# Strided attention: dense weights over four heads, values masked on GpSimd, 2 KiB store runs

## The chip, the cores and the metric

The kernel runs on one core of one Trainium2 chip. The metric is device time in microseconds of the whole program, median over its executions. The profile lists the instructions of TensorE (PE, 880 matmuls in the kernel before, with its 880 weight loads as PEld), VectorE (DVE, 144), ScalarE (ACT, 103), GpSimd (POOL, 23) and SyncE (SP) apart, and the packets of 16 DMA engines, which in the kernel before read 25.95 MB from HBM and wrote 25.17 MB to it. "Span" is the time from the first to the last instruction of the profiled execution; it is about 1.8 us shorter than the device time here.

## The reference

Every query attends to 16 fixed key positions, every 64th row of K and V:

```python
batch, heads, seq, dim = (8, 12, 1024, 64)
attend_positions = np.arange(0, seq, stride)            # stride = 64: 16 keys
scores = np.einsum('bhqd,bhkd->bhqk', q, k) * scale     # scale = 1/sqrt(64)
weights = np.exp(scores - np.max(scores, axis=-1, keepdims=True))
weights = weights / (np.sum(weights, axis=-1, keepdims=True) + 1e-10)
result[:, :, i, :] = np.einsum('bhqk,bhkd->bhqd', weights, v)[:, :, 0, :]
```

Q and the result are float32, 25.2 MB each. The arithmetic is small; nearly all traffic is one read of Q and one write of the result.

## The kernel before

The 96 (batch, head) pairs are done in 24 groups of four heads. A group's Q is one DMA of 1 MiB, each partition holding 32 rows (8 KiB); its result is one DMA of 1 MiB. Loads run 11 groups ahead (`QBUFS`), and nine output buffers (`OBUFS`) hold results on their way out. All DMAs are issued by SP, in the order of the code.

```python
def scores(g):                      # [cut: the four score matmuls into sc]
    w = wt[g] = w_bufs[g % 3]       # zeroed once; half of each block stays zero
    for a in range(2):
        wa = w[64 * a : 64 * a + 64]
        nc.scalar.activation(
            out=_ap_with(wa, [wa.ap[0], [P, 8], [1, 2], [2, 32]], extra_offset=64 * a),
            in_=sc[64 * a : 64 * a + 64].rearrange("p (t x q) -> p t x q", t=8, x=2),
            func=AF.Exp, bias=0.0, scale=scale,
        )

def outputs(g, c):                  # four times a group
    ps = psum_o.tile([P, 2, 2, 2 * D], FP32, name="o_ps", tag="o")
    for i in range(2):
        nc.tensor.matmul(ps[:, :, i], lhsT=wt[g][:, 2 * c + i],
                         rhs=v_bd[:, g // 2, g % 2].rearrange("p s d -> p (s d)"), ...)
    nc.vector.tensor_tensor(out=out_sb[g][:, :, 4 * c : 4 * c + 4], in0=ps, ... rec[g] ..., op=ALU.mult)

def store(g):                       # per partition: two runs of 16 rows = 4 KiB, one read of 8 KiB
    o = out_sb[g]
    _copy(nc,
        _ap_with(out, [[16 * D, P], [2 * SD, 2], [1, 16 * D]], g * HG * SD),
        _ap_with(o, [o.ap[0], [1, 1], [1, 32 * D]]))

for g in range(NG):                 # steady loop
    sums(g); outputs(g, 0); outputs(g, 1)
    if g + 1 < NG: scores(g + 1)
    outputs(g, 2)
    if g + 2 < NG: transposes(g + 2, 0)
    outputs(g, 3)
    if g + 2 < NG: transposes(g + 2, 1)
    store(g)
    if g + QBUFS < NG: load(g + QBUFS)
```

The softmax here doesn't subtract the row's maximum and nothing guards it: scores larger than these inputs give would overflow.

Of the kernel before, what the change touches and what calls it, by code (L numbers as in the profile page):

```python
# [11 lines left out]
FP32 = mybir.dt.float32  # L12
BF16 = mybir.dt.bfloat16
I16 = mybir.dt.int16
AF = mybir.ActivationFunctionType
ALU = mybir.AluOpType


def _ap_with(ap: bass.AP, new_ap, extra_offset: int = 0) -> bass.AP:
    return dataclasses.replace(  # L20
        ap, ap=[list(p) for p in new_ap], offset=ap.offset + extra_offset
    )
# [26 lines left out]
def kernel(  # L49
# [8 lines left out]
    nc = tc.nc  # L58

    B, H, S, D = Q.shape  # L60
    NK = S // stride
    scale = 1.0 / math.sqrt(D)

    P = 128
    HG = 4
    NG = B * H // HG
    NC = NG // 2
    SD = S * D
# [4 lines left out]
    const = ctx.enter_context(tc.tile_pool(name="const", bufs=1))  # L73
    qn_pool = ctx.enter_context(tc.tile_pool(name="qn", bufs=QBUFS))
    out_pool = ctx.enter_context(tc.tile_pool(name="outsb", bufs=OBUFS))
    qt_pool = ctx.enter_context(tc.tile_pool(name="qt", bufs=2))
    rec_pool = ctx.enter_context(tc.tile_pool(name="rec", bufs=2))
    psum_qt = ctx.enter_context(tc.tile_pool(name="pqt", bufs=2, space=bass.MemoryType.PSUM))
    psum_sc = ctx.enter_context(tc.tile_pool(name="psc", bufs=2, space=bass.MemoryType.PSUM))
# [23 lines left out]

    identity = const.tile([P, P], BF16, name="identity")
    make_identity(nc, identity)
    id_v = identity.rearrange("p (c b a k) -> p c b a k", c=2, b=2, a=2)

    perm_k = const.tile([P, 2, 2, 2, NK], BF16, name="perm_k")

    perm_v = const.tile([P, 2, 2, 2, 2, NK], BF16, name="perm_v")  # L110
    for c in range(2):
        for a in range(2):
            nc.gpsimd.tensor_copy(out=perm_k[:, c, a], in_=id_v[:, c, :, a])
    k_dup = const.tile([P, NC, 2, D], BF16, name="k_dup")
    for e in range(2):
        nc.gpsimd.tensor_copy(out=k_dup[:, :, e], in_=k_raw)  # L116
    for c in range(2):
        for a in range(2):
            for e in range(2):
                nc.gpsimd.tensor_copy(  # L120
                    out=perm_v[:, c, a, :, e], in_=id_v[:, c, :, a]
                )
    v_bf = const.tile([P, NC, D], BF16, name="v_bf")
    nc.gpsimd.tensor_copy(out=v_bf, in_=v_raw)  # L124

    k_t = const.tile([P, NC, 2, 4, 2, NK], BF16, name="k_t")
    nc.vector.memset(k_t, 0.0)  # L127
    w_bufs = []
    for i in range(3):
        w = const.tile([P, 8, P], BF16, name=f"w{i}")  # L130
        nc.vector.memset(w, 0.0)
        w_bufs.append(w)


    iota_p = const.tile([P, 1], I16, name="iota_p")
    nc.gpsimd.iota(iota_p, pattern=[[0, 1]], base=0, channel_multiplier=1)  # L136
    slot_i = const.tile([P, 1], I16, name="slot_i")
    nc.vector.tensor_scalar(  # L138
        out=slot_i, in0=iota_p, scalar1=4, scalar2=3,
        op0=ALU.logical_shift_right, op1=ALU.bitwise_and,  # L140
    )
    slot_f = const.tile([P, 1], FP32, name="slot_f")
    nc.vector.tensor_copy(out=slot_f, in_=slot_i)
    col4 = const.tile([P, 4], I16, name="col4")
    nc.gpsimd.iota(col4, pattern=[[1, 4]], base=0, channel_multiplier=0)
    s_sel = const.tile([P, 4], BF16, name="s_sel")
    nc.vector.tensor_scalar(
        out=s_sel, in0=col4, scalar1=slot_f, scalar2=None, op0=ALU.is_equal
    )
    mask = const.tile([P, 4], FP32, name="mask")  # L150
    nc.vector.tensor_scalar(
        out=mask, in0=col4, scalar1=slot_f, scalar2=None, op0=ALU.is_equal
    )


    pk = perm_k.rearrange("p c a b k -> p (c a b k)")
    for n in range(NC // 4):
        kp = psum_o.tile([P, 4, 2, 4, NK], FP32, name="kp", tag="o")
        for i in range(4):
            nc.tensor.matmul(  # L160
                kp[:, i], lhsT=k_dup[:, 4 * n + i].rearrange("p e d -> p (e d)"),
                rhs=pk, start=True, stop=True,
            )
        for e in range(2):
            h = slice(64 * e, 64 * e + 64)
            nc.scalar.copy(  # L166
                k_t[h, 4 * n : 4 * n + 4, :, :, e].rearrange("p n c s k -> p (n c s) k"),
                kp[h].rearrange("p n c s k -> p (n c s) k"),
            )

    v_bd = const.tile([P, NC, 2, 4, D], BF16, name="v_bd")
    for n in range(2):
        for c in range(2):
            vp = psum_sc.tile([P, NC // 2, D], FP32, name="vp", tag="sc")
            nc.tensor.matmul(  # L175
                vp, lhsT=perm_v[:, c].rearrange("p a b e k -> p (a b e k)"),
                rhs=v_bf[:, 6 * n : 6 * n + 6], start=True, stop=True,
            )
            for s in range(4):
                nc.vector.tensor_scalar(  # L180
                    out=v_bd[:, 6 * n : 6 * n + 6, c, s], in0=vp,
                    scalar1=mask[:, s : s + 1], scalar2=None, op0=ALU.mult,
                )

    qt, wt, rec, out_sb = {}, {}, {}, {}

    def transposes(g, x):
        if x == 0:
            qt[g] = qt_pool.tile([P, 2, 8, P], BF16, name="qt", tag="qt")
        ps = psum_qt.tile([P, 8, P], BF16, name="qt_ps", tag="qt_ps")  # L190
        qb = qn[g].bitcast(BF16)
        for i in range(8):
            nc.tensor.transpose(  # L193
                ps[:, i],
                _ap_with(qb, [qb.ap[0], [2, P]], extra_offset=(8 * x + i) * 2 * P + 1),
                identity,
            )
        nc.scalar.copy(qt[g][:, x], ps)  # L198

    def scores(g):  # L200
        sc = psum_sc.tile([P, 512], FP32, name="sc", tag="sc")
        q = qt[g]
        kt = k_t[:, g // 2, g % 2].rearrange("p s e k -> p (s e k)")
        for j in range(4):
            a, b = divmod(j, 2)
            nc.tensor.matmul(  # L206
                sc[32 * j : 32 * j + 32],
                lhsT=kt[:, 32 * j : 32 * j + 32],
                rhs=_ap_with(
                    q, [q.ap[0], [P, 8], [8 * P, 2], [1, 32]],  # L210
                    extra_offset=32 * (2 * b + a),
                ),
                start=True, stop=True, tile_position=(0, 32 * j),
            )
        w = wt[g] = w_bufs[g % 3]
        for a in range(2):
            wa = w[64 * a : 64 * a + 64]
            nc.scalar.activation(  # L218
                out=_ap_with(wa, [wa.ap[0], [P, 8], [1, 2], [2, 32]], extra_offset=64 * a),
                in_=sc[64 * a : 64 * a + 64].rearrange("p (t x q) -> p t x q", t=8, x=2),  # L220
                func=AF.Exp, bias=0.0, scale=scale,
            )

    def sums(g):
        sm = psum_s.tile([P, 2, 8, 2], FP32, name="sm", tag="sm")
        for i in range(8):
            nc.tensor.matmul(  # L227
                sm[:, :, i], lhsT=wt[g][:, i], rhs=s_sel, start=True, stop=True
            )
        rec[g] = rec_pool.tile([P, 2, 16], FP32, name="rec", tag="rec")  # L230
        nc.vector.reciprocal(rec[g], sm.rearrange("p b i e -> p b (i e)"))  # L231

    def outputs(g, c):
        if c == 0:
            out_sb[g] = out_pool.tile([P, 2, 16, D], FP32, name="out_sb", tag="out_sb")
        ps = psum_o.tile([P, 2, 2, 2 * D], FP32, name="o_ps", tag="o")
        for i in range(2):
            nc.tensor.matmul(  # L238
                ps[:, :, i], lhsT=wt[g][:, 2 * c + i],
                rhs=v_bd[:, g // 2, g % 2].rearrange("p s d -> p (s d)"),  # L240
                start=True, stop=True,
            )
        nc.vector.tensor_tensor(  # L243
            out=out_sb[g][:, :, 4 * c : 4 * c + 4],
            in0=ps.rearrange("p b i (e d) -> p b (i e) d", e=2),
            in1=rec[g][:, :, 4 * c : 4 * c + 4].unsqueeze(3).to_broadcast([P, 2, 4, D]),
            op=ALU.mult,
        )

    def store(g):  # L250
        o = out_sb[g]
        _copy(
            nc,
            _ap_with(out, [[16 * D, P], [2 * SD, 2], [1, 16 * D]], g * HG * SD),
            _ap_with(o, [o.ap[0], [1, 1], [1, 32 * D]]),
        )

    for g in range(2):
        for x in range(2):
            transposes(g, x)  # L260
    scores(0)
    for g in range(NG):
        sums(g)
        outputs(g, 0)
        outputs(g, 1)
        if g + 1 < NG:
            scores(g + 1)
        outputs(g, 2)
        if g + 2 < NG:
            transposes(g + 2, 0)  # L270
        outputs(g, 3)
        if g + 2 < NG:
            transposes(g + 2, 1)
        store(g)
        if g + QBUFS < NG:
            load(g + QBUFS)
# [35 lines left out]
```

## Time and profile before

| | before |
|---|---|
| device time, median | 130.34 us (130.26 to 130.61, 4 runs) |
| span of the profiled run | 128.5 us |
| bytes moved, mean rate | 51.26 MB, 399 GB/s |
| busy: PE, DVE, ACT, POOL | 54%, 65%, 67%, 4% |
| last compute instruction ends | about 114 us |

First the page of the kernel before: the span in 40 slices. A digit is the busy share of the 16 DMA engines in tenths, and below it is the rate that they reached.

```profile
span 128.5 us, 2215 instructions
...
DMA  2999989999899899999999999999998999999980
GB/s 57 351 398 418 449 367 490 388 423 439 339 421 487 357 441 439 413 434 449 383 467 426 393 459 428 393 469 421 405 469 357 416 434 416 421 428 421 434 337 23
DMA packets 7722, 51.26 MB, mean 399 GB/s; under 512 B 3872, under 2 KB 3872, under 8 KB 3872
```

The engines are 80% busy or more, mostly over 90%, from the second slice to the third from last. The queue part of the same page (packets, megabytes, share of 16 engines' span) has one data queue, and two small ones that carry instructions.

```profile
q1 hardware_dynamic: 7712, 51.12, 96.3%
q8 instruction: 7, 0.11, 0.4%
q14 instruction: 3, 0.02, 0.0%
```

The table of stretches of the same trace: per stretch the busy time of each engine, then PE's granted clock, the DMA share and the rate.

```profile
core 0: us, PE busy (x) PEld busy (x) DVE busy (x) ACT busy (x) POOL busy (x), PEclk, DMA share, GB/s
60.00:70.00 10.00, 6.29 (x85) 4.51 (x82) 7.65 (x13) 8.44 (x10) 0.00 (x0) 1.00 1.04 440
110.00:115.00 5.00, 1.41 (x16) 0.89 (x16) 3.82 (x7) 0.83 (x2) 0.00 (x0) 0.80 1.02 424
115.00:120.00 5.00, 0.00 (x0) 0.00 (x0) 0.00 (x0) 0.00 (x0) 0.00 (x0) 0.50 1.01 423
120.00:125.00 5.00, 0.00 (x0) 0.00 (x0) 0.00 (x0) 0.00 (x0) 0.00 (x0) 0.50 0.92 385
125.00:128.50 3.50, 0.00 (x0) 0.00 (x0) 0.00 (x0) 0.00 (x0) 0.00 (x0) 0.50 0.09 37
```

The DMA share stays at 1.0 when compute has ended (115 to 120 us), at 423 GB/s, against 440 and 424 GB/s in the two stretches above it. The chain of waits tells another story if it is read alone:

```profile
ACT 60%; PE 13%; DVE 5%; DMA 3%; POOL 3%; issue 2%; ACTq 1%; DVEq 0%; POOLq 0%
ACT qt L198 34%; ACT w L218 26%; PE sc L206 8%; DVE v_bd L180 3%; DMA k_raw<-in_K_dram 3%; PE qt_ps L193 2%; PE o_ps L238 2%; DVE out_sb L243 1%; POOL k_dup L116 1%; POOL perm_v L120 1%; PE sm L227 1%; POOL v_bf L124 1%; ACTq L307 1%; DVEq 
```

It follows ACT because it goes from each instruction to what released it, and loads that landed early release nothing (the list of waits has no wait of a compute engine for a load of Q). It does not say that ACT limits the time: on the chain one group follows the other every 3.94 us, while its load and store take the DMA engines about 4.95 us (an estimate: 2.097 MB at 424 GB/s). The groups of instructions behind it (busy time, mean ns, idle time before and its releaser):

```profile
L243 DVE TENSOR_TENSOR out_sb<-o_ps,rec 128x512 f32<-128x512 f32 x96 | 63.3, 688 | 15.3 <-PE o_ps L238 12.9
L198 ACT COPY qt<-qt_ps 128x1024 bf16<-128x1024 bf16 x48 | 46.2, 1015 | 5.2 <-PE qt_ps L193 4.7
L218 ACT ACTIVATE w<-sc 64x512 bf16<-64x512 f32 x48 | 35.4, 737 | 13.2 <-PE sc L206 12.9
```

Last, two lines on SP. Its timeline (start us, us, what) has the first store:

```profile
25.18 0.63 SPq L34 DMA_DIRECT2D out_dram<-out_sb  x1
```

Its list of waits (us in total, times, longest us) has the wait for the last stores, at the end of the program:

```profile
SPq L307 <- DMA out_dram<-out_sb: 12.6, 1, 12.6
```

### The profile page before, as it was taken

The numbers are of one execution on the slowest core, as the hardware profiler recorded it, in microseconds if no ns is written. First come the engines' busy times: TensorE is split into PE (matmuls) and PEld (weight loads), VectorE is DVE, ScalarE is ACT, GpSimd is POOL, SyncE is SP. The second block draws the span as 40 slices with busy tenths as digits, with TensorE's granted clock in tenths as the row PEclk, the third lists the DMA queues.
The fourth block names the chain that finished last, engine by engine and source line by source line (L and its number), as shares of the span: only waits on it lengthen the run. The fifth ranks groups of instructions, "written<-read, shape, count | busy, mean of one in ns | idle before, by whom it ended". The sixth has DMA issues, their size and how long they took to land.

```text
span 128.5 us, 2215 instructions
## 1 busy us (share of the span) xinstructions
PE 69.4 (54%) x880; PEld 51.1 (40%) x880; DVE 83.7 (65%) x144; ACT 86.3 (67%) x103; POOL 5.1 (4%) x23
## 2 busy tenths in 40 slices
PE   0071665975656866558766578665687655510000
PEld 0040542754445654445544456443465444300000
DVE  6229963787677777787777877877877778750000
ACT  2163294988889888898888898888988888400000
POOL 4470000000000000000000000000000000000000
PEclk9999997799999999999999999999999999955555
DMA  2999989999899899999999999999998999999980
GB/s 57 351 398 418 449 367 490 388 423 439 339 421 487 357 441 439 413 434 449 383 467 426 393 459 428 393 469 421 405 469 357 416 434 416 421 428 421 434 337 23
DMA packets 7722, 51.26 MB, mean 399 GB/s; under 512 B 3872, under 2 KB 3872, under 8 KB 3872
## 3 DMA queue, kind: packets, MB, share of 16 engines
q1 hardware_dynamic: 7712, 51.12, 96.3%
q8 instruction: 7, 0.11, 0.4%
q14 instruction: 3, 0.02, 0.0%
HBM read 25.95 MB, written 25.17 MB: 398 GB/s over the span
## 4 chain that ended last, share of the span: by engine, by line
ACT 60%; PE 13%; DVE 5%; DMA 3%; POOL 3%; issue 2%; ACTq 1%; DVEq 0%; POOLq 0%
ACT qt L198 34%; ACT w L218 26%; PE sc L206 8%; DVE v_bd L180 3%; DMA k_raw<-in_K_dram 3%; PE qt_ps L193 2%; PE o_ps L238 2%; DVE out_sb L243 1%; POOL k_dup L116 1%; POOL perm_v L120 1%; PE sm L227 1%; POOL v_bf L124 1%; ACTq L307 1%; DVEq L307 0%; PE vp L175 0%
## 5 line engine op out<-in xcount | busy, mean ns | idle before, releaser
L243 DVE TENSOR_TENSOR out_sb<-o_ps,rec 128x512 f32<-128x512 f32 x96 | 63.3, 688 | 15.3 <-PE o_ps L238 12.9
L198 ACT COPY qt<-qt_ps 128x1024 bf16<-128x1024 bf16 x48 | 46.2, 1015 | 5.2 <-PE qt_ps L193 4.7
L218 ACT ACTIVATE w<-sc 64x512 bf16<-64x512 f32 x48 | 35.4, 737 | 13.2 <-PE sc L206 12.9
L238 PE MATMUL o_ps<-v_bd,w 128*128 128x256 bf16 x192 | 33.4, 278 | 0.6 <-DVE out_sb L243 0.6
L193 PE MATMUL qt_ps<-identity,qn 128*128 128x128 bf16 x384 | 30.7, 227 | 0.2 <-ACT qt L198 0.2
L193 PEld LDWEIGHTS <-qn 128*128 128x128 bf16 x384 | 27.0, 102 | 3.9 <-issue 2.6
L206 PE MATMUL sc<-qt,k_t 128*32 128x512 bf16 x96 | 9.8, 395 | 24.5 <-ACT qt L198 24.5
L238 PEld LDWEIGHTS <-w 128*128 128x128 bf16 x192 | 14.3, 98 | 6.9 <-issue 6.2
L206 PEld LDWEIGHTS <-k_t 128*32 128x32 bf16 x96 | 4.4, 93 | 29.3 <-issue 29.2
L231 DVE RECIPROCAL rec<-sm 128x32 f32<-128x32 f32 x24 | 8.6, 358 | 9.0 <-PE sm L227 9.0
L227 PE MATMUL sm<-s_sel,w 128*128 128x4 bf16 x192 | 8.5, 166 | 6.9 <-ACT w L218 6.9
L227 PEld LDWEIGHTS <-w 128*128 128x128 bf16 x192 | 6.4, 96 | 11.0 <-ACT w L218 11.0
L180 DVE TENSOR_SCALAR v_bd<-vp,mask 128x384 bf16<-128x384 f32 x16 | 8.5, 608 | 0.1
L166 ACT CAST k_t<-kp 64x512 bf16<-64x512 f32 x6 | 3.5, 579 | 3.6 <-PE kp L160 3.5
L160 PE MATMUL kp<-perm_k,k_dup 128*128 128x128 bf16 x12 | 1.5, 312 | 6.7 <-POOL k_dup L116 6.7
L175 PE MATMUL vp<-v_bf,perm_v 128*128 128x384 bf16 x4 | 1.8, 490 | 4.6 <-DVE v_bd L180 4.1
L160 PEld LDWEIGHTS <-k_dup 128*128 128x128 bf16 x12 | 1.2, 145 | 6.7 <-POOL k_dup L116 6.7
L138 DVE TENSOR_SCALAR slot_i<-iota_p 128x1 int16<-128x1 int16 x1 | 0.2, 156 | 4.7 <-POOL iota_p L136 4.7
L166 ACT ACT_TABLE_LOAD x1 | 1.3, 1283 | 2.5 <-DVE k_t L127 2.5
L127 DVE MEMSET k_t<- 128x1536 uint32 x1 | 1.3, 1338 | 1.1 <-PEq L293 1.1
L175 PEld LDWEIGHTS <-perm_v 128*128 128x128 bf16 x4 | 0.5, 127 | 3.7 <-issue 3.7
L116 POOL CAST k_dup<-k_raw 128x768 bf16<-128x768 f32 x2 | 1.6, 827 | 3.0 <-DMA k_raw<-in_K_dram 3.0
(15 smaller groups left out, 6.0 us busy)
## 6 DMA issues: line engine op xcount, KB each, us to landing
qn<-in_Q_dram SPq DMA_DIRECT2D x24, 1024.0 KB, 19.0
out_dram<-out_sb SPq DMA_DIRECT2D x24, 1024.0 KB, 19.5
k_raw<-in_K_dram SPq DMA_DIRECT2D x1, 384.0 KB, 4.3
v_raw<-in_V_dram SPq DMA_DIRECT2D x1, 384.0 KB, 5.4
```

What stands on the lines that cost most here:

```text
L116: nc.gpsimd.tensor_copy(out=k_dup[:, :, e], in_=k_raw)
L160: nc.tensor.matmul(kp[:, i], lhsT=k_dup[:, 4 * n + i].rearrange("p e d -> p (e d)"), rhs=pk, start=True, stop=True,)
L166: nc.scalar.copy(k_t[h, 4 * n : 4 * n + 4, :, :, e].rearrange("p n c s k -> p (n c s) k"), kp[h].rearrange("p n c s k -> p (n c s) k"),)
L180: nc.vector.tensor_scalar(out=v_bd[:, 6 * n : 6 * n + 6, c, s], in0=vp, scalar1=mask[:, s : s + 1], scalar2=None, op0=ALU.mult,)
L193: nc.tensor.transpose(ps[:, i], _ap_with(qb, [qb.ap[0], [2, P]], extra_offset=(8 * x + i) * 2 * P + 1), identity,)
L198: nc.scalar.copy(qt[g][:, x], ps)
L206: nc.tensor.matmul(sc[32 * j : 32 * j + 32], lhsT=kt[:, 32 * j : 32 * j + 32], rhs=_ap_with(q, [q.ap[0], [P, 8], [8 * P, 2], [1, 32]], ext ...
L218: nc.scalar.activation(out=_ap_with(wa, [wa.ap[0], [P, 8], [1, 2], [2, 32]], extra_offset=64 * a), in_=sc[64 * a : 64 * a + 64].rearrange( ...
L227: nc.tensor.matmul(sm[:, :, i], lhsT=wt[g][:, i], rhs=s_sel, start=True, stop=True)
L231: nc.vector.reciprocal(rec[g], sm.rearrange("p b i e -> p b (i e)"))
L238: nc.tensor.matmul(ps[:, :, i], lhsT=wt[g][:, 2 * c + i], rhs=v_bd[:, g // 2, g % 2].rearrange("p s d -> p (s d)"), start=True, stop=True,)
L243: nc.vector.tensor_tensor(out=out_sb[g][:, :, 4 * c : 4 * c + 4], in0=ps.rearrange("p b i (e d) -> p b (i e) d", e=2), in1=rec[g][:, :, 4 ...
```

## The change

The intent: the same weights block serves all four heads (four full blocks of 128 columns instead of eight half-zero ones), so that sums and outputs take half the matmuls and weight loads, and one exp does for two. The heads must then be told apart on the side of the values, which are masked per group, on GpSimd. Each output partition now holds 8 rows of each of four heads instead of 16 rows of two, so a store writes four runs of 2 KiB per 8 KiB read. The core of the diff (cut: setup, names, loop arguments):

```diff
-    v_bd = const.tile([P, NC, 2, 4, D], BF16, name="v_bd")      # 16 masked copies in setup
+    v_rep = const.tile([P, NC, 2, D], BF16, name="v_rep")       # 4 plain copies in setup
+    def values(g):
+        vb[g] = vb_pool.tile([P, 8, D], BF16, name="vb", tag="vb")
+        nc.gpsimd.tensor_tensor(
+            out=vb[g], in0=mask,
+            in1=v_rep[:, g // 2, g % 2].unsqueeze(1).to_broadcast([P, 8, D]),
+            op=ALU.mult,
+        )
...
-        w = wt[g] = w_bufs[g % 3]
-        for a in range(2):
-            wa = w[64 * a : 64 * a + 64]
-            nc.scalar.activation(
-                out=_ap_with(wa, [wa.ap[0], [P, 8], [1, 2], [2, 32]], extra_offset=64 * a),
-                in_=sc[64 * a : 64 * a + 64].rearrange("p (t x q) -> p t x q", t=8, x=2),
+        w = wt[g] = w_pool.tile([P, 4, P], BF16, name="w", tag="w")
+        nc.scalar.activation(
+            out=_ap_with(w, [w.ap[0], [1, 4], [P, 4], [4, 32]]),
+            in_=sc.rearrange("p (q s r) -> p q s r", q=4, s=4),
...
-        for i in range(2):
-            nc.tensor.matmul(ps[:, :, i], lhsT=wt[g][:, 2 * c + i], rhs=v_bd[...], ...)
+        nc.tensor.matmul(ps, lhsT=wt[g][:, s], rhs=vb[g], ...)
...
-            _ap_with(out, [[16 * D, P], [2 * SD, 2], [1, 16 * D]], g * HG * SD),
+            _ap_with(out, [[8 * D, P], [SD, 4], [1, 8 * D]], g * HG * SD),
```

More of the change, by code (lines that the diff above doesn't have):

```diff
@@ L76 @@
     qt_pool = ctx.enter_context(tc.tile_pool(name="qt", bufs=2))
+    w_pool = ctx.enter_context(tc.tile_pool(name="w", bufs=2))
+    vb_pool = ctx.enter_context(tc.tile_pool(name="vb", bufs=3))
     rec_pool = ctx.enter_context(tc.tile_pool(name="rec", bufs=2))
@@ L105 @@
     make_identity(nc, identity)
-    id_v = identity.rearrange("p (c b a k) -> p c b a k", c=2, b=2, a=2)
-    perm_k = const.tile([P, 2, 2, 2, NK], BF16, name="perm_k")
-    perm_v = const.tile([P, 2, 2, 2, 2, NK], BF16, name="perm_v")
-    for c in range(2):
-        for a in range(2):
-            nc.gpsimd.tensor_copy(out=perm_k[:, c, a], in_=id_v[:, c, :, a])
+    id_v = identity.rearrange("p (c h k) -> p c h k", c=2, h=4)
     k_dup = const.tile([P, NC, 2, D], BF16, name="k_dup")
@@ L116 @@
         nc.gpsimd.tensor_copy(out=k_dup[:, :, e], in_=k_raw)
-    for c in range(2):
-        for a in range(2):
-            for e in range(2):
-                nc.gpsimd.tensor_copy(
-                    out=perm_v[:, c, a, :, e], in_=id_v[:, c, :, a]
-                )
+    perm_v = const.tile([P, 2, 4, 2, NK], BF16, name="perm_v")
+    for e in range(2):
+        nc.gpsimd.tensor_copy(out=perm_v[:, :, :, e], in_=id_v)
     v_bf = const.tile([P, NC, D], BF16, name="v_bf")
     nc.gpsimd.tensor_copy(out=v_bf, in_=v_raw)
-    k_t = const.tile([P, NC, 2, 4, 2, NK], BF16, name="k_t")
+    k_t = const.tile([P, NG, 4, 2, NK], BF16, name="k_t")
     nc.vector.memset(k_t, 0.0)
-    w_bufs = []
-    for i in range(3):
-        w = const.tile([P, 8, P], BF16, name=f"w{i}")
-        nc.vector.memset(w, 0.0)
-        w_bufs.append(w)
     iota_p = const.tile([P, 1], I16, name="iota_p")
@@ L138 @@
     nc.vector.tensor_scalar(
-        out=slot_i, in0=iota_p, scalar1=4, scalar2=3,
-        op0=ALU.logical_shift_right, op1=ALU.bitwise_and,
+        out=slot_i, in0=iota_p, scalar1=4, scalar2=None, op0=ALU.logical_shift_right
     )
@@ L143 @@
     nc.vector.tensor_copy(out=slot_f, in_=slot_i)
-    col4 = const.tile([P, 4], I16, name="col4")
-    nc.gpsimd.iota(col4, pattern=[[1, 4]], base=0, channel_multiplier=0)
-    s_sel = const.tile([P, 4], BF16, name="s_sel")
+    col8 = const.tile([P, 8], I16, name="col8")
+    nc.gpsimd.iota(col8, pattern=[[1, 8]], base=0, channel_multiplier=0)
+    s_sel = const.tile([P, 8], BF16, name="s_sel")
     nc.vector.tensor_scalar(
-        out=s_sel, in0=col4, scalar1=slot_f, scalar2=None, op0=ALU.is_equal
+        out=s_sel, in0=col8, scalar1=slot_f, scalar2=None, op0=ALU.is_equal
     )
-    mask = const.tile([P, 4], FP32, name="mask")
-    nc.vector.tensor_scalar(
-        out=mask, in0=col4, scalar1=slot_f, scalar2=None, op0=ALU.is_equal
-    )
-    pk = perm_k.rearrange("p c a b k -> p (c a b k)")
+    mask = const.tile([P, 8, D], BF16, name="mask")
+    nc.vector.tensor_copy(out=mask, in_=s_sel.unsqueeze(2).to_broadcast([P, 8, D]))
     for n in range(NC // 4):
-        kp = psum_o.tile([P, 4, 2, 4, NK], FP32, name="kp", tag="o")
+        kp = psum_o.tile([P, 4, 8, NK], FP32, name="kp", tag="o")
         for i in range(4):
@@ L161 @@
                 kp[:, i], lhsT=k_dup[:, 4 * n + i].rearrange("p e d -> p (e d)"),
-                rhs=pk, start=True, stop=True,
+                rhs=identity, start=True, stop=True,
             )
@@ L166 @@
             nc.scalar.copy(
-                k_t[h, 4 * n : 4 * n + 4, :, :, e].rearrange("p n c s k -> p (n c s) k"),
-                kp[h].rearrange("p n c s k -> p (n c s) k"),
+                k_t[h, 8 * n : 8 * n + 8, :, e].rearrange("p g h k -> p (g h) k"),
+                kp[h].rearrange("p n c k -> p (n c) k"),
             )
-    v_bd = const.tile([P, NC, 2, 4, D], BF16, name="v_bd")
+    v_rep = const.tile([P, NC, 2, D], BF16, name="v_rep")
     for n in range(2):
@@ L175 @@
             nc.tensor.matmul(
-                vp, lhsT=perm_v[:, c].rearrange("p a b e k -> p (a b e k)"),
+                vp, lhsT=perm_v[:, c].rearrange("p h e k -> p (h e k)"),
                 rhs=v_bf[:, 6 * n : 6 * n + 6], start=True, stop=True,
             )
-            for s in range(4):
-                nc.vector.tensor_scalar(
-                    out=v_bd[:, 6 * n : 6 * n + 6, c, s], in0=vp,
-                    scalar1=mask[:, s : s + 1], scalar2=None, op0=ALU.mult,
-                )
-    qt, wt, rec, out_sb = {}, {}, {}, {}
+            nc.vector.tensor_copy(out=v_rep[:, 6 * n : 6 * n + 6, c], in_=vp)
+    qt, wt, vb, out_sb = {}, {}, {}, {}
+    def values(g):
[5 more added lines that the diff above has]
+        )
     def transposes(g, x):
         if x == 0:
-            qt[g] = qt_pool.tile([P, 2, 8, P], BF16, name="qt", tag="qt")
+            qt[g] = qt_pool.tile([P, 16, P], BF16, name="qt", tag="qt")
         ps = psum_qt.tile([P, 8, P], BF16, name="qt_ps", tag="qt_ps")
@@ L197, in transposes @@
             )
-        nc.scalar.copy(qt[g][:, x], ps)
+        nc.scalar.copy(qt[g][:, 8 * x : 8 * x + 8], ps)
     def scores(g):
         sc = psum_sc.tile([P, 512], FP32, name="sc", tag="sc")
-        q = qt[g]
-        kt = k_t[:, g // 2, g % 2].rearrange("p s e k -> p (s e k)")
-        for j in range(4):
-            a, b = divmod(j, 2)
+        for h in range(4):
             nc.tensor.matmul(
-                sc[32 * j : 32 * j + 32],
-                lhsT=kt[:, 32 * j : 32 * j + 32],
-                rhs=_ap_with(
-                    q, [q.ap[0], [P, 8], [8 * P, 2], [1, 32]],
-                    extra_offset=32 * (2 * b + a),
-                ),
-                start=True, stop=True, tile_position=(0, 32 * j),
-            )
@@ L215, in scores @@
-        w = wt[g] = w_bufs[g % 3]
-        for a in range(2):
-            wa = w[64 * a : 64 * a + 64]
-            nc.scalar.activation(
-                out=_ap_with(wa, [wa.ap[0], [P, 8], [1, 2], [2, 32]], extra_offset=64 * a),
-                in_=sc[64 * a : 64 * a + 64].rearrange("p (t x q) -> p t x q", t=8, x=2),
-                func=AF.Exp, bias=0.0, scale=scale,
-            )
-    def sums(g):
-        sm = psum_s.tile([P, 2, 8, 2], FP32, name="sm", tag="sm")
-        for i in range(8):
-            nc.tensor.matmul(
-                sm[:, :, i], lhsT=wt[g][:, i], rhs=s_sel, start=True, stop=True
-            )
-        rec[g] = rec_pool.tile([P, 2, 16], FP32, name="rec", tag="rec")
-        nc.vector.reciprocal(rec[g], sm.rearrange("p b i e -> p b (i e)"))
@@ L233, in outputs @@
-    def outputs(g, c):
-        if c == 0:
-            out_sb[g] = out_pool.tile([P, 2, 16, D], FP32, name="out_sb", tag="out_sb")
-        ps = psum_o.tile([P, 2, 2, 2 * D], FP32, name="o_ps", tag="o")
-        for i in range(2):
-            nc.tensor.matmul(
-                ps[:, :, i], lhsT=wt[g][:, 2 * c + i],
-                rhs=v_bd[:, g // 2, g % 2].rearrange("p s d -> p (s d)"),
-                start=True, stop=True,
-            )
+                sc[32 * h : 32 * h + 32],
+                lhsT=k_t[:, g, h].rearrange("p e k -> p (e k)"),
@@ new lines, in scores @@
+                rhs=qt[g][:, :, 32 * h : 32 * h + 32],
+                start=True, stop=True, tile_position=(0, 32 * h),
+            )
+        w = wt[g] = w_pool.tile([P, 4, P], BF16, name="w", tag="w")
+        nc.scalar.activation(
+            out=_ap_with(w, [w.ap[0], [1, 4], [P, 4], [4, 32]]),
+            in_=sc.rearrange("p (q s r) -> p q s r", q=4, s=4),
+            func=AF.Exp, bias=0.0, scale=scale,
+        )
+    def sums(g):
+        sm = psum_s.tile([P, 4, 8], FP32, name="sm", tag="sm")
+        for s in range(4):
+            nc.tensor.matmul(sm[:, s], lhsT=wt[g][:, s], rhs=s_sel, start=True, stop=True)
+        rec = rec_pool.tile([P, 4, 8], FP32, name="rec", tag="rec")
+        nc.vector.reciprocal(rec, sm)
+        return rec
@@ L243, in outputs @@
+    def outputs(g, s, rec):
+        if s == 0:
+            out_sb[g] = out_pool.tile([P, 4, 4, 2, D], FP32, name="out_sb", tag="out_sb")
+        ps = psum_o.tile([P, 4, 2, D], FP32, name="o_ps", tag="o")
+        nc.tensor.matmul(
+            ps.rearrange("p h e d -> p (h e d)"), lhsT=wt[g][:, s],
+            rhs=vb[g].rearrange("p s d -> p (s d)"), start=True, stop=True,
+        )
         nc.vector.tensor_tensor(
-            out=out_sb[g][:, :, 4 * c : 4 * c + 4],
-            in0=ps.rearrange("p b i (e d) -> p b (i e) d", e=2),
@@ L246, in outputs @@
-            in1=rec[g][:, :, 4 * c : 4 * c + 4].unsqueeze(3).to_broadcast([P, 2, 4, D]),
+            out=out_sb[g][:, :, s], in0=ps,
+            in1=rec[:, s].rearrange("p (h e) -> p h e", e=2)
+            .unsqueeze(3).to_broadcast([P, 4, 2, D]),
             op=ALU.mult,
@@ L258 @@
     for g in range(2):
+        values(g)
         for x in range(2):
@@ L262 @@
     for g in range(NG):
-        sums(g)
-        outputs(g, 0)
-        outputs(g, 1)
+        rec = sums(g)
+        outputs(g, 0, rec)
+        outputs(g, 1, rec)
         if g + 1 < NG:
             scores(g + 1)
-        outputs(g, 2)
+        outputs(g, 2, rec)
         if g + 2 < NG:
+            values(g + 2)
             transposes(g + 2, 0)
-        outputs(g, 3)
+        outputs(g, 3, rec)
         if g + 2 < NG:
```

## The prediction

> What bounds the kernel now. The slices of the page show the 16 DMA engines 90% busy or more from the third slice to the third from last. The table of stretches gives a DMA share of about 1.0 and 410 to 441 GB/s in nearly every stretch from 5 to 120 us, 424 GB/s from 110 us, where only stores are left. So DMA throughput binds: 51.26 MB at 424 GB/s is 121 us, plus a head of 4 us and a ragged tail. The chain of waits names ACT (60% of the span), but that is not the limit: a group takes 3.94 us there (two 1.02 us copies, two 0.74 us exps, a 0.42 us wait for scores), while its 2.1 MB of load and store need 4.94 us of DMA. Compute ends at 114 us; the core then waits 12.6 us for stores.
>
> What the change does.
> - ACT: one 128x512 exp for two 64x512 ones, 0.74 us less a group (17.7 us in all).
> - DVE: per group the same (four 0.69 us multiplies, one 0.36 us reciprocal: 3.1 us). In setup, 16 masked copies (8.5 us) become four plain ones, an estimated 2 us.
> - PE: half the weight loads and matmuls for sums and outputs.
> - POOL: a new 128x512 two-input multiply per group. [...] No trace here shows it yet.
> - DMA: same loads, bytes and number of stores. Each 8 KiB read of a store now feeds four 2 KiB writes instead of two 4 KiB ones.
>
> All but the last is off the critical path. Compute's group period may fall from 3.94 to about 3.3 us and the first store go out some 5 us earlier (25.2 to about 20 us), but the DMA engines have no idle time to fill between 5 and 123 us, so none of it is gained.
>
> On the critical path: the price of a store packet. In the trace's DMA records 8 KiB of a store take 312 ns on an engine, and a 32 KiB load packet (written in 8 KiB pieces) 1219 ns beside stores, 305 per 8 KiB. [...] Two more pieces per store packet cost an estimated 4.5 ns (fitted from load and store packets here)[...]. Each engine moves 192 store packets: 0.9[...] us more. The 256-byte K and V packets take about 18 ns, 9 over their bytes, which as an upper bound would make it 3.3 us.
>
> Predicted time: 131.4 us (130.4 plus about 1.0), range 130.1 to 133.0. Faster by over 2%: 0.03; within 2%: 0.85; slower by over 2%: 0.12.
>
> What shows each step: store packets of about 317 ns and some 418 GB/s while only stores run; DMA share still 1.0; first store near 20 us; 24 exps of about 0.74 us; ACT busy near 68 us; a longer final wait for stores.
>
> What would make it wrong: 2 KiB writes spread over four heads costing HBM much more than the overhead (a clearly slower store-only stretch); the POOL multiply taking over 4 us, so that compute falls behind the DMA; or an earlier start changing how loads and stores mix, making packets dearer or cheaper.

The sum was 130.4 us plus about 1.0 us, 131.4 us. Of the 1.0 us, about 0.9 us follows from what is printed, as the author's estimate: 192 store packets at 4.5 ns.

## The result

The changed kernel takes 130.96 us (130.89 to 131.09, 4 runs) against 130.34 us: ratio 1.0045, 95% interval 1.0028 to 1.0063. Executions over 1.5% slower than the fastest of the same kernel are left out of the means. A ratio here is the mean time of one kernel's runs over that of the other's of the same rounds, so it is not quite the ratio of the medians quoted. So the kernel is a little slower, by 0.6 us, within the 2% that counts as the same. The views of the changed kernel that answer to those above follow. First the slices:

```profile
span 129.1 us, 1842 instructions
...
DMA  2999989999899999899999899999998999999980
GB/s 56 350 396 416 447 365 487 396 411 447 320 429 457 386 429 454 378 457 426 391 459 439 373 449 434 391 464 398 411 472 360 414 421 424 411 424 424 411 365 25
DMA packets 7720, 51.23 MB, mean 397 GB/s; under 512 B 3872, under 2 KB 3872, under 8 KB 3872
```

The DMA engines are as full as before, at 397 GB/s for 399. The queues:

```profile
q1 hardware_dynamic: 7712, 51.12, 96.5%
q8 instruction: 5, 0.08, 0.2%
q14 instruction: 3, 0.02, 0.0%
```

There are five 16 KB instruction packets for seven; TensorE has fewer instructions (687 matmuls and 688 weight loads for 880 of each). The stretches:

```profile
core 0: us, PE busy (x) PEld busy (x) DVE busy (x) ACT busy (x) POOL busy (x), PEclk, DMA share, GB/s
60.00:70.00 10.00, 6.68 (x74) 3.68 (x72) 8.17 (x14) 8.33 (x10) 3.40 (x3) 1.00 1.00 422
110.00:115.00 5.00, 0.00 (x0) 0.00 (x0) 0.00 (x0) 0.00 (x0) 0.00 (x0) 0.50 1.01 419
115.00:120.00 5.00, 0.00 (x0) 0.00 (x0) 0.00 (x0) 0.00 (x0) 0.00 (x0) 0.50 1.01 419
120.00:125.00 5.00, 0.00 (x0) 0.00 (x0) 0.00 (x0) 0.00 (x0) 0.00 (x0) 0.50 1.00 416
125.00:128.50 3.50, 0.00 (x0) 0.00 (x0) 0.00 (x0) 0.00 (x0) 0.00 (x0) 0.50 0.20 84
```

With only stores left (115 to 120 us), the rate is 419 GB/s where it was 423. The chain and the groups:

```profile
DMA 33%; ACT 29%; PE 9%; DVE 5%; issue 4%; POOL 2%; DVEq 1%; ACTq 0%
DMA out_dram<-out_sb 30%; ACT qt L187 20%; ACT w L199 8%; PE sc L192 4%; DVE out_sb L221 4%; DMA k_raw<-in_K_dram 3%; PE qt_ps L182 3%; POOL k_dup L111 1%; PE o_ps L217 1%; PE vp L159 1%; POOL v_bf L117 1%; DVE rec L210 1%; DVEq L287 0%; DV
...
L221 DVE TENSOR_TENSOR out_sb<-o_ps,rec 128x512 f32<-128x512 f32 x96 | 63.2, 689 | 17.7 <-PE o_ps L217 13.9
L187 ACT COPY qt<-qt_ps 128x1024 bf16<-128x1024 bf16 x48 | 48.2, 1051 | 4.4 <-PE qt_ps L182 4.2
L170 POOL TENSOR_TENSOR vb<-mask,v_rep 128x512 bf16<-128x512 bf16 x24 | 27.6, 1153 | 62.0 <-PE o_ps L217 60.3
L199 ACT ACTIVATE w<-sc 128x512 bf16<-128x512 f32 x24 | 31.7, 1322 | 14.1 <-PE sc L192 14.1
```

The chain now names the stores first, because compute, started earlier, now has to wait for output buffers (DVE three times, 1.8 us in all; never in the kernel before). The exp (L199) takes 1322 ns each, which the prediction had at 0.74 us; the GpSimd multiply takes 1153 ns. SP's first store in its timeline:

```profile
20.89 0.63 SPq L34 DMA_DIRECT2D out_dram<-out_sb  x1
```

It went out 4.3 us earlier, and the time did not fall. The wait for the last stores:

```profile
SPq L287 <- DMA out_dram<-out_sb: 11.4, 1, 11.4
```

It is 1.2 us shorter, though the stores end no earlier: SP came to it later, at 116.3 us for 115.3.

Three quantities which the views do not print come from the trace's DMA and semaphore records. The mean length of an 8 KiB store packet was 312.2 ns before and is 316.2 ns. The last store is finished by its 16 engines one after the other, over 3.29 us before and 2.50 us in the changed kernel, and SP's wait for it ends 0.02 us after the slowest in both. And from the last landing to the last instruction of the program passes some more time ("end"):

```text
last store, us from the span's start: mean over 16 engines, slowest engine; then the end
before   mean 125.38  slowest 127.50  end 1.00   span 128.50
after    mean 126.25  slowest 127.64  end 1.50   span 129.14
```

The mean moved by 0.87 us, just under the predicted 0.9 us. But the span moved by 0.14 us through the slowest engine and by 0.50 us through the end. So the right total came about in another way than the prediction says, and that was what to test. One profiled execution each is little, but the spans of all fast executions agree: their mean is 128.6 us before (11 runs) and 129.2 us after (4 runs). Taking off the ends above, which assumes that they are the same in every execution, leaves an estimated 127.6 and 127.7 us for the slowest engine.

### The profile page after: what moved, and what is told of

It reads as the page before. It is cut to its first block, busy times and chain, and to the rows that moved or that the text cites. A ratio compares the mean times of both kernels' runs of the same rounds, so it can differ in the third digit from the quotient of the medians.

```text
span 129.1 us, 1842 instructions
## 1 busy us (share of the span) xinstructions
PE 69.4 (54%) x687; PEld 41.0 (32%) x688; DVE 75.7 (59%) x129; ACT 80.1 (62%) x79; POOL 31.3 (24%) x37
## 3 DMA queue, kind: packets, MB, share of 16 engines
q1 hardware_dynamic: 7712, 51.12, 96.5%
## 4 chain that ended last, share of the span: by engine, by line
DMA 33%; ACT 29%; PE 9%; DVE 5%; issue 4%; POOL 2%; DVEq 1%; ACTq 0%
DMA out_dram<-out_sb 30%; ACT qt L187 20%; ACT w L199 8%; PE sc L192 4%; DVE out_sb L221 4%; DMA k_raw<-in_K_dram 3%; PE qt_ps L182 3%; POOL k_dup L111 1%; PE o_ps L217 1%; PE vp L159 1%; POOL v_bf L117 1%; DVE rec L210 1%; DVEq L287 0%; DVE v_rep L163 0%; POOL perm_v L115 0%
## 5 line engine op out<-in xcount | busy, mean ns | idle before, releaser
L187 ACT COPY qt<-qt_ps 128x1024 bf16<-128x1024 bf16 x48 | 48.2, 1051 | 4.4 <-PE qt_ps L182 4.2
L170 POOL TENSOR_TENSOR vb<-mask,v_rep 128x512 bf16<-128x512 bf16 x24 | 27.6, 1153 | 62.0 <-PE o_ps L217 60.3
L199 ACT ACTIVATE w<-sc 128x512 bf16<-128x512 f32 x24 | 31.7, 1322 | 14.1 <-PE sc L192 14.1
L182 PE MATMUL qt_ps<-identity,qn 128*128 128x128 bf16 x384 | 32.6, 235 | 4.2 <-DMA qn<-in_Q_dram 3.9
L217 PE MATMUL o_ps<-vb,w 128*128 128x512 bf16 x95 | 34.1, 401 | 0.7 <-DVE out_sb L221 0.7
L182 PEld LDWEIGHTS <-qn 128*128 128x128 bf16 x384 | 28.2, 106 | 11.6 <-DMA qn<-in_Q_dram 5.2
L217 PEld LDWEIGHTS <-w 128*128 128x128 bf16 x96 | 7.6, 98 | 5.9 <-issue 5.6
L208 PE MATMUL sm<-s_sel,w 128*128 128x8 bf16 x96 | 6.2, 170 | 4.1 <-ACT w L199 3.1
L208 PEld LDWEIGHTS <-w 128*128 128x128 bf16 x96 | 4.4, 99 | 7.9 <-ACT w L199 7.9
L144 PE MATMUL kp<-identity,k_dup 128*128 128x128 bf16 x12 | 1.5, 312 | 6.7 <-POOL k_dup L111 6.7
L163 DVE CAST v_rep<-vp 128x384 bf16<-128x384 f32 x4 | 2.0, 552 | 0.1
```

What stands on the lines that cost most here:

```text
L170: nc.gpsimd.tensor_tensor(out=vb[g], in0=mask, in1=v_rep[:, g // 2, g % 2].unsqueeze(1).to_broadcast([P, 8, D]), op=ALU.mult,)
L182: nc.tensor.transpose(ps[:, i], _ap_with(qb, [qb.ap[0], [2, P]], extra_offset=(8 * x + i) * 2 * P + 1), identity,)
L187: nc.scalar.copy(qt[g][:, 8 * x : 8 * x + 8], ps)
L199: nc.scalar.activation(out=_ap_with(w, [w.ap[0], [1, 4], [P, 4], [4, 32]]), in_=sc.rearrange("p (q s r) -> p q s r", q=4, s=4), func=AF.Ex ...
L208: nc.tensor.matmul(sm[:, s], lhsT=wt[g][:, s], rhs=s_sel, start=True, stop=True)
L217: nc.tensor.matmul(ps.rearrange("p h e d -> p (h e d)"), lhsT=wt[g][:, s], rhs=vb[g].rearrange("p s d -> p (s d)"), start=True, stop=True,)
```

## The experiments

The theory at the outset: only the number of write pieces in a store packet costs time. The rivals: the new compute, above all the GpSimd multiply, costs it; or the scatter of the pieces over four heads does. Twelve kernels were run. "Wrong on purpose" means that the output is misplaced or wrong in value, while the work timed stays the same.

| run | median us | ratio to before (95%) | store packet ns | slowest engine, end us |
|---|---|---|---|---|
| changed kernel | 130.96 | 1.0045 (1.0028 to 1.0063) | 316.2 | 127.64, 1.50 |
| b_2k | 130.59 | 1.0025 (1.0005 to 1.0044) | 316.1 | 127.80, 1.01 |
| a_4k | 130.35 | 0.9999 (0.9984 to 1.0015) | 312.2 | 127.06, 1.48 |
| a_8k | 130.29 | 0.9992 (0.9977 to 1.0007) | 310.3 | 127.05, 1.51 |
| a_2kadj | 130.99 | 1.0040 (1.0024 to 1.0057) | 315.7 | 127.77, 1.48 |
| a_nopool | 130.50 | 1.0005 (0.9988 to 1.0022) | 315.9 | 127.70, 1.01 |
| a_dve | 130.95 | 1.0044 (1.0028 to 1.0059) | 316.7 | 127.39, 1.00 |
| b_ms48 | 130.21 | 0.9985 (0.9972 to 0.9998) | 312.0 | 127.35, 1.02 |
| dma_free | 127.63 | 0.9791 (0.9778 to 0.9803) | 311.0 | 124.75, 1.06 |
| dma_fetch | 129.36 | 0.9918 (0.9902 to 0.9935) | 311.8 | 126.92, 1.06 |
| a_512 | 172.07, four of six runs slow | 1.3007 (1.2956 to 1.3058), two runs | 337.6 | 171.58, 1.50 |
| dma_only (faulty) | 184.63 | 1.4163 (1.4116 to 1.4210) | 309.3 | 180.89, 1.08 |
| a_expcontig | 130.96, one run | not known | 316.0 | 127.69, 1.50 |

The last two columns are of one profiled execution each. How they move between executions of one kernel was not recorded; the spans move by some tenths (128.7 to 129.5 us in the six of b_2k). Mean span less the end gives, as an estimate by the same assumption as above, 127.9 us for the slowest engine of b_2k and 127.1 us for a_4k.

### b_2k: the old compute with the new store

```diff
# kernel before; rows land in the wrong place on purpose
-            _ap_with(out, [[16 * D, P], [2 * SD, 2], [1, 16 * D]], g * HG * SD),
+            _ap_with(out, [[8 * D, P], [SD, 4], [1, 8 * D]], g * HG * SD),
```

> The kernel before with the store pattern of the changed kernel: four 2 KiB writes per 8 KiB read (rows land in the wrong place on purpose, all of the output is written once). Theory (only the count of write pieces per store packet costs time, compute is off the path): store packets 316 ns as in the changed kernel (312 before), total 130.9 to 131.1 us, ratio about 1.005. Rival (the new compute order, or the GpSimd multiply[...], costs the 0.6 us): 130.3 to 130.5 us, ratio within 0.001 of 1.

Measured: 130.59 us, ratio 1.0025, between the two expectations; packets 316.1 ns as the theory said. The pieces do cost time by themselves, but less than the whole 0.6 us, as far as the interval can tell.

### a_4k and a_8k: the new compute with fewer pieces

```diff
# changed kernel; wrong place on purpose
-            _ap_with(out, [[8 * D, P], [SD, 4], [1, 8 * D]], g * HG * SD),
+            _ap_with(out, [[16 * D, P], [2 * SD, 2], [1, 16 * D]], g * HG * SD),   # a_4k
+            _ap_with(out, [[32 * D, P], [1, 1], [1, 32 * D]], g * HG * SD),        # a_8k
```

> The changed kernel with the store pattern of before: two 4 KiB writes per read (wrong place on purpose). Theory: store packets 312 ns, total 130.2 to 130.4 us, ratio 0.999 to 1.001. Rival (compute or GpSimd costs the time): 130.9 to 131.1 us.

> The changed kernel with one contiguous 8 KiB write per read (wrong place on purpose). Theory with 2.0 ns per write piece: store packets about 310 ns, total about 129.9 us, ratio 0.996 to 0.998, and shorter issues on the queue of SP. Rival: unchanged at 130.9 to 131.1 us.

Measured: 130.35 us for a_4k (packets 312.2 ns) as the theory said: with all of the new compute in place, the old store pattern brings the old time. That does not put the rival out. Against the kernel before, the end is 0.48 us longer and the slowest engine 0.44 us earlier, so two effects of the new compute cancel here; a_nopool below takes them apart. For a_8k the packets are 310.3 ns as expected, the rate from 118 to 123 us is 429 GB/s (419 in the changed kernel, 424 in a_4k, but also 428 in the kernel before, so that this rate tells little), but the total is 130.29 us where 129.9 was expected, a small miss: the mean over engines did not fall, as its load packets were longer (1246 ns against 1237 in a_4k: 48 of them an engine make 0.43 us, and 192 store packets save 0.36 us). Why they were longer is open. The stretch of a_8k, columns as above:

```profile
118.00:123.00 5.00, 0.00 (x0) 0.00 (x0) 0.00 (x0) 0.00 (x0) 0.00 (x0) 0.50 1.02 429
```

SP's issues became short again too: the median store took SP 516 ns here and 591 in a_4k, for 1881 ns in the changed kernel. So SP is held up at its issues with four pieces per packet. That this costs nothing while the engines have work was argued, not shown.

### a_2kadj: the four pieces side by side

```diff
# changed kernel; wrong place on purpose
-            _ap_with(out, [[8 * D, P], [SD, 4], [1, 8 * D]], g * HG * SD),
+            _ap_with(out, [[32 * D, P], [8 * D, 4], [1, 8 * D]], g * HG * SD),
```

> The changed kernel with the four 2 KiB writes of a packet side by side in memory, one 8 KiB run cut in four (wrong place on purpose). Theory (the count of pieces costs, not where they lie): store packets 316 ns, total 130.9 to 131.1 us. Rival (it is the scatter over four heads, 256 KiB apart, that costs in HBM): store packets 310 to 312 ns, total 129.9 to 130.4 us.

Measured: 130.99 us, packets 315.7 ns. The count of pieces costs, not where they lie; the scatter over heads is out.

### a_512: sixteen pieces

```diff
# changed kernel; wrong place on purpose
-            _ap_with(out, [[8 * D, P], [SD, 4], [1, 8 * D]], g * HG * SD),
+            _ap_with(out, [[2 * D, P], [SD // 4, 16], [1, 2 * D]], g * HG * SD),
```

> The changed kernel with sixteen scattered 512-byte writes per 8 KiB read (wrong place on purpose). Theory, a constant 2.0 ns per piece: store packets 308 + 16 x 2 = 340 ns, 24 ns x 192 packets = 4.6 us more than the changed kernel, 135.5 us, ratio to before 1.04. The bound taken in the prediction from the 256-byte packets (9 ns per piece pair) would give some 400 ns and 147 us. [...]

Measured: 168.92 and 170.31 us in two runs (172.07 us is the median with the four slow ones), ratio 1.3007, far over either figure. The store packets took 337.6 ns, near the 340 ns that the constant price of 2.0 ns per piece gives (this profile was of a run marked slow, 174.85 us, 3.5% above this kernel's fastest, so the figure is only roughly comparable). The load packets, which were not changed, took 1706 ns for 1239. They did so in dma_only as well (1697 ns), whose engines also stood idle in between (79.9% of their span filled), so packet lengths of a run with a nearly empty queue are no sure price of a piece. The rest of the loss is waiting: the DMA queue ran dry (by the trace's DMA records, single microseconds with under a tenth of the engines busy), which does not happen in the kernel before or the changed one (85% busy or more in every microsecond from 3 to 124 us). SP was inside one issue or another for 151 of the 173 us and could not issue fast enough. Its loads here (min, median, max ns of one issue):

```profile
L34 SPq DMA_DIRECT2D qn<-in_Q_dram x24: 472/5508/14646, 2.0 to 125.6; - x24
```

The median over all 24 loads is 5.5 us, against 0.55 us in the kernel before. The 13 loads behind such a store held SP for 5.4 to 14.6 us, 7.6 us in the median, where a group of load and store has about 4.95 us. What inside the issue takes the time was not tested. So the small price per piece does not foretell the time at any size: with 2 KiB pieces the data packets filled 96.5% of the 16 engines' span, with 512 B pieces 87.4%, and the engines waited while SP was issuing.

### dma_only and dma_free: no compute at all

```diff
# kernel before, loop replaced; wrong values on purpose
-        o = out_sb[g]
+        o = qn[g]        # dma_only: store the loaded Q tile
+        o = filler       # dma_free: store one constant tile, filled once
...
+    for g in range(NG):
+        store(g)
+        if g + QBUFS < NG: load(g + QBUFS)
```

> The kernel before with no compute in its loop: each group's Q tile is stored back as it came (wrong values on purpose), same loads and stores with 4 KiB runs, setup kept. Theory (DMA-bound): 129.5 to 131 us, no faster than before by more than 1%, store packets 312 ns. Rival (the chain of ACT and PE sets part of the time, as the chain of waits says): clearly faster, under 125 us.

Measured: 184.63 us, ratio 1.4163. This was a fault of the experiment. Load g + 11 reuses the buffer that store g has just begun to read, and SP issues in order, so it stood there until the store had landed (8.8 us from issue to landing in the median). Three lines of its timeline (start us, us, what) show a pair every 9 us:

```profile
45.59 0.47 SPq L34 DMA_DIRECT2D qn<-in_Q_dram  x1
46.11 0.59 SPq L34 DMA_DIRECT2D out_dram<-qn  x1
54.83 0.47 SPq L34 DMA_DIRECT2D qn<-in_Q_dram  x1
```

It says nothing about compute. The repair stores a constant tile, so that no DMA waits for another's buffer:

> Repair of the run without compute: its stores read one constant tile, so neither stores nor loads wait on each other (wrong values on purpose); setup kept, 4 KiB runs as before. Theory (DMA-bound): no more than 1% faster than before, 129.2 to 130.5 us, packets of 312 ns. Rival (the chain of ACT and PE sets part of the time): under 127 us.

Measured: 127.63 us, ratio 0.9791. This lies between the two expectations, and the theory's "no more than 1%" is wrong: 2.7 us of the kernel before go away with its compute, although its DMA engines looked full. The mean over engines of the last landing moved only from 125.38 to 124.47 us; the slowest engine moved from 127.50 to 124.75 us. The 16 engines now finish within 0.5 us of each other, for 3.3 us before. The queue part of its page shows what else is gone:

```profile
q1 hardware_dynamic: 7712, 51.12, 98.2%
```

There are no instruction packets in it; its profile has 187 instructions, for 2215 in the kernel before.

### dma_fetch: instructions without data

```diff
# dma_free (wrong values on purpose), plus:
+    tick = psum_s.tile([P, P], FP32, name="tick", tag="sm")
+    for _ in range(872):
+        nc.tensor.matmul(tick[0:1], lhsT=identity[0:1, 0:1], rhs=identity[0:1], start=True, stop=True)
```

> The run without compute (127.6 us, last store landing on all 16 DMA engines within 0.5 us of each other, no instruction fetches in the trace), with 872 matmuls of one row added on TensorE: about as many TensorE instructions as the kernel before has (1762), hardly any data. What made the kernel before 2.8 us slower than the run without compute? Theory (TensorE's own instructions are fetched by the same DMA engines, 16 KB at a time, and a fetch holds one of the 16 back by some 1.5 us, so that the slowest engine ends late): about 7 fetches of 16 KB in the trace, the last store's landings spread over 2 to 3 us, total 129.3 to 130.4 us. Rival (the data traffic of compute in SBUF and PSUM slows the DMA): no such spread, total 127.5 to 128.0 us.

Measured: 129.36 us, ratio 0.9918, within the theory's range, and its queues:

```profile
q1 hardware_dynamic: 7712, 51.12, 96.7%
q8 instruction: 7, 0.11, 0.3%
```

Seven fetches of 16 KB, the last landings spread over 2.6 us, the slowest engine at 126.92 us. (This profile is of the slowest of four executions: its span is 128.0 us, the others have 127.4 to 127.6.) So TensorE's instruction stream alone, with hardly any data, costs 1.7 of the 2.7 us (127.63 to 129.36 us). The fetches show in the trace as packets of 16,384 bytes on q8: 7 in the kernel before, with 880 matmuls and 880 weight loads, and 5 in the changed one, with 687 and 688; the other instruction queue, q14, had packets of 8 KB. A 16 KB fetch beside the data takes about 1.03 us, and at the first of them one DMA engine falls behind. In the kernel before the first fetch is at 27.2 us: of the DMA that lands next, the slowest engine is 1.47 us behind the second slowest, where the DMA ahead of it had them level (0.00 us). In dma_fetch, whose loop has no other compute, the first fetch at 24.5 us makes the same step, from 0.01 to 1.18 us.

For the last 1.0 us to the kernel before, its trace has a clue. Its landings are spread over some 2.3 us up to the DMA that lands at 99.5 us. From the next one on, after an 8 KB fetch on q14 at 99.8 us, the spread grows within five DMAs to 3.34 us. b_ms48 does the same after its fetch at 99.9 us (2.23 to 3.22 us); dma_fetch, with the same stores and no such fetch, stays at 2.65 us. Why the spread goes on growing when the fetch itself took 0.31 us is not shown, and neither is that the traffic of compute has no part.

### a_nopool, a_dve and b_ms48: the GpSimd multiplies

```diff
# a_nopool: changed kernel, masked values of groups 0 to 2 used for all (wrong values on purpose)
+        if g >= 3:
+            vb[g] = vb[g % 3]
+            return
# a_dve: changed kernel
-        nc.gpsimd.tensor_tensor(
+        nc.vector.tensor_tensor(
# b_ms48: kernel before, after its setup
+    for _ in range(48):
+        nc.gpsimd.memset(pad, 0.0)          # pad is [128, 1]
```

> The changed kernel with the masked values made for the first three groups only and used again for all (wrong values on purpose): 21 of 24 GpSimd multiplies gone. Theory: 130.9 to 131.1 us as the changed kernel; the qt copies fall from 1051 ns back to about 1015 if GpSimd traffic slows ACT, else stay. Rival (GpSimd multiply costs the 0.6 us): 130.3 us.

Measured: 130.50 us, ratio 1.0005: the rival's figure, nearly. Yet store packets are still 315.9 ns and the slowest engine is still at 127.70 us. What fell is the end, from 1.50 to 1.01 us. The copies did not fall back either (1051 ns as in the changed kernel), so GpSimd's traffic is not what lengthened them. The end is 1.48 to 1.51 us in all six profiles with 24 GpSimd multiplies, and 1.00 to 1.08 us in the eight without them or with three of them; within it the trace shows GpSimd's first drain after the last wait take 211 ns and begin 0.44 us after the semaphore instruction ahead of it began, for 77 ns and 0.09 us in the kernel before.

> The changed kernel with the masked values made on the vector engine instead of GpSimd (right result). In the profiles so far the last store lands 0.14 us later in the changed kernel (127.64 against 127.50 us) and the end of the program after that takes 1.50 us in every kernel with 24 GpSimd multiplies and 1.00 us in those with 0 or 3. New theory: most of the 0.6 us is this longer end. Then here: end 1.00 us, total 130.4 to 130.6 us, ratio 1.000 to 1.002. Rival (packet cost alone sets the time): 130.9 to 131.1 us. Also tells if 24 more vector operations of 128x512 bf16 fit under the DMA time: DVE busy some 8 to 15 us more, no effect on the total.

Measured: 130.95 us, ratio 1.0044. The end is 1.00 us as expected, and the mean span of six runs, 128.75 us, is 0.4 us under the changed kernel's 129.2. But the total did not fall: device time exceeds the span by 2.10 to 2.19 us in this kernel, by 1.79 to 1.81 us in the changed one. What lies outside the span no view shows; this gain was given back there, and why stays open. That 24 more vector operations fit in without a longer span was right: they took 416 ns each.

> The kernel before with 48 one-column memsets on GpSimd after its setup, done long before the end (right result). If the mere length of GpSimd's program lengthens the end (its next instructions have to be fetched), the end grows from 1.00 to about 1.50 us and the total to 130.8 to 130.9 us (ratio 1.004). If it takes multiplies, or work late in the run, it stays 1.00 us and 130.3 to 130.5 us.

Measured: 130.21 us, end 1.02 us. So 48 more GpSimd instructions, done by 16 us, do not lengthen the end; whether it is the multiplies as such or work late in the run was not tried. Nor is an instruction fetch ruled out as its cause. In all six profiles with the longer end, and in none of the others, an 8 KB fetch on q14 begins 0.04 to 0.21 us after the last instruction (0.05 us in the changed kernel); in b_ms48 the extra fetch came long before. This run shows one fetch more, of 8 KB, at 15.7 us: the slowest engine, level with the second (0.02 us) one DMA before, is 0.52 us behind it in the next.

### a_expcontig: the step of the exp's writes

```diff
# changed kernel; wrong columns on purpose
-            out=_ap_with(w, [w.ap[0], [1, 4], [P, 4], [4, 32]]),
-            in_=sc.rearrange("p (q s r) -> p q s r", q=4, s=4),
+            out=w.rearrange("p s m -> p (s m)"),
+            in_=sc,
```

> The changed kernel with the exp writing its 512 columns side by side instead of 4 apart (wrong columns on purpose). The exp took 1.32 us in the changed kernel where I expected 0.74. If the step of 8 bytes between written elements is the cause, the exp falls to 0.7 to 0.8 us; if the cause is 128 partitions for 64, it stays at 1.3 us. Total about 131 us either way, as ACT is off the path.

Measured (one look, state unknown): total 130.96 us, and the exp

```profile
L187 ACT COPY qt<-qt_ps 128x1024 bf16<-128x1024 bf16 x48 | 46.6, 1014 | 18.0 <-PE qt_ps L182 17.9
...
L199 ACT ACTIVATE w<-sc 128x512 bf16<-128x512 f32 x24 | 14.3, 598 | 14.3 <-PE sc L192 14.3
```

takes 598 ns for 1322. So the way it wrote, in steps of 8 bytes, cost 0.72 us an exp, and the number of partitions is not the cause. (The edit also takes away the jump after each 32 elements; the exp of the kernel before, with steps of 4 bytes and runs of 32, took 737 ns on half the partitions, so that the step is the likelier part.) The copies between the exps took 1014 ns again, for 1051, so their slowness went with the exp's writes. More than halving ACT's busy time on this line (31.7 to 14.3 us) moved the total by nothing, as far as one run can tell.

## Why the prediction was right or wrong

The forecast of "about the same, about 1 us slower" held: 130.96 us for a predicted 131.4, within the range.

- DMA bounds the kernel, and cheaper or earlier compute is not gained: shown by dma_free (with no compute at all the time falls by 2.1% only) and by a_expcontig (ACT busy for 65.6 us instead of 80.1, the same 130.96 us, in one run). a_4k (all of the new compute, old store: 130.35 us against 130.38) agrees, though as the sum of two effects that cancel.
- "Two more pieces per store packet cost an estimated 4.5 ns (fitted from load and store packets here)": measured 4.0 ns (312.2 to 316.2), so 2.0 ns per piece, 1.9 from one piece to two, and roughly 1.8 on to sixteen (337.6 ns in the slow profile of a_512). The fit set a mean (312 ns) beside a median: the 1219 ns of a load packet is the median, its mean was 1239 ns. That the count does it and not the scatter is shown by a_2kadj.
- "Each engine moves 192 store packets: 0.9 ... us more": 192 x 4.0 ns is 0.77 us, and the mean engine ended 0.87 us later. As a sum over engines this term was right in kind and a little too large. The step that fails is taking it over to the time one for one. The last store ends with the slowest engine, and that one moved by 0.14 us. Between a_4k and the changed kernel, which differ in the store alone, the total moved by 0.6 us; between the kernel before and b_2k by 0.2 us in the medians. With the old store, the new compute drew the slowest engine in by 0.44 us (127.50 before, 127.06 in a_4k). That the changed kernel fetches two blocks of 16 KB less is not enough as a reason: b_2k fetches seven like the kernel before, and its slowest engine too moved by 0.30 us only, with a mean 0.95 us later. The traces show where the rest went. At the DMA that lands near 100 us, the slowest engine is still as far behind the mean in both kernels, 1.32 us before and 1.42 us after. At the end it is 2.12 and 1.40 us: in the kernel before, the growth described under dma_fetch comes in between, after the fetch at 99.8 us. In all six kernels with 2 KiB pieces that fetch comes later, at 107.0 to 107.3 us, and the distance changes by 0.11 us or less from 100 us to the end. So part of the price was hidden by a loss of the kernel before that the changed one does not have. That this fetch is the cause is argued from the times, not tested.
- A term was missing: the longer end of the program with 24 GpSimd multiplies, 0.50 us, which a_nopool takes away with 0.46 us of the time (130.96 to 130.50 us); in a_dve the end went too and the time did not. By luck it took the place of what the slowest engine did not pay, so the sum came out near.
- "The DMA engines have no idle time to fill between 5 and 123 us, so none of it is gained" is right of idle time (no slice of the page there is under 80% busy), but "full" did not mean "all useful and evenly spread": dma_free shows 2.7 us that compute costs, 1.7 of them with TensorE's instructions and their fetches.
- POOL: 1.15 us a multiply measured. First store near 20 us: 20.9 us. Store-only rate some 418 GB/s: 419.
- Exp groups of about 0.74 us and ACT busy near 68 us: wrong, 1.32 us and 80.1 us, because of the step of the writes. "A longer final wait for stores": wrong, 11.4 us for 12.6, as SP was held up at the issue of the last store (3.1 us, for 0.5 us before), and so began its final wait later. Neither was on the critical path.

No run that gives the right result beat the kernel before by more than 0.2%.

## What to carry to other kernels

When the table of stretches shows the DMA share at 1.0 also where no compute runs, as here (1.01 at 423 GB/s), cost a change by what it does to the DMA packets, and expect little from cheaper engines, whatever the chain of waits names: here all compute of the loop together was worth 2.1% (dma_free). Then look at the slowest of the 16 DMA engines rather than at their mean: here an engine fell behind by 1.2 to 1.6 us at the first instruction fetch (1.47 us before, 1.57 after, 1.18 in dma_fetch), and the run that adds TensorE instructions, with seven fetches, to a loop without compute took 1.7 us longer (127.63 to 129.36 us). A run with all compute taken out, and with no new waits put in, measures how much there is to win.
